# GpSimd runs the S5 parameter chain, with reordered loads, products and sums, in a hybrid decoder layer

## The chip, the cores and the metric

The kernel runs on one core of one Trainium2 chip. The metric is the device time of one execution in microseconds (us). Engines: PE is TensorE (matmul), DVE is VectorE, ACT is ScalarE, POOL is GpSimd, and SP is SyncE, which only issues transfers.

## The reference

One layer of a hybrid decoder with D = 1024 channels and T = 1024 tokens, batch 1, all in float32. x is normalised, projected by one matrix of 4352 columns, and split into an RWKV-7 branch (512 wide, 8 heads of 64), an S5 branch (512 wide, 32 groups of 16 channels, 64 complex states each) and two gates. The branches are merged, projected and added to x; a gated MLP with a causal convolution of width 3 (22 tiles of 128 hidden channels a half) follows.

```python
h = rms_norm(x, norm_mix_pre);  proj = h @ w_in
p_rwkv, u_s5, gates = split(proj);  gates = sigmoid(gates + b_gate)
o_rwkv = rwkv7_branch(p_rwkv, ...) @ w_branch_rwkv     # token shift, decay, delta rule scan, norm, gate
o_s5 = s5_branch(u_s5, ...) @ w_branch_s5
x = x + rms_norm((g_rwkv * o_rwkv + g_s5 * o_s5) @ w_out, norm_mix_post)
h = rms_norm(x, norm_ffn_pre)
f = conv_ffn(h, w_up, conv_w, conv_b, w_down)          # gelu(gate) * val after the convolution
x = x + rms_norm(f, norm_ffn_post)

# s5_branch
lam = a_re + 1j * a_im;  dt = exp(log_step)[:, None]
a_bar = exp(lam * dt)
b_bar = ((a_bar - 1) / lam)[..., None] * (b_re + 1j * b_im)
# states = scan of  s_t = a_bar * s_(t-1) + b_bar u_t ;  y = Re(c . states) + d * u ; gelu ; glu
```

What the change calls the S5 parameter chain is `a_bar`, `(a_bar - 1) / lam` and powers of `a_bar`, per group and state: arrays of 128 partitions by 32.

## The kernel before

**Products.** Float32 is kept by splitting each operand into a rounded high part and a low part, and by three matmuls for each product: high times high, high times low, low times high. Tiles are 128x128 (weights) by 128x512 (half of the tokens). The token halves are th = 0 and 1. The program needs 9040 matmuls. `split` makes the two parts with a cast on ACT (L164, L234) and a subtraction on DVE (L165, L235).

**Order.** PE's order is the order of the program text (`manual_schedule` for PE). In the mixing stage a small planner writes it: *lanes* are generators that yield a cost and a latency, `drive` runs the lane step whose latency is over, and fills the time between with projection products (*background* or *fill*), by the numbers `T_...`, `PACE` and `CREDIT` at the end of the file. The order on DVE, ACT, POOL and SP is a scheduler's, which follows priorities (`high_priority(HP)`, `HP2`, `HPW`, `HPN`: larger goes first). Each engine then runs its own queue strictly in order; a transfer is issued by the engine that is named in the code, and stands in that engine's queue.

**The start.** `start` loads x (8 tiles of 256 KB per half) and four tiles of w_in, twice. For each of 8 blocks k it makes `hh` (ACT, L1015) and `hl` (DVE, L1016), then 4 x 3 products go into the four banks gm (L1083 to L1085). In parallel the squares `sq` of x are summed (ACT L1021, DVE L1023, L1025), PE adds them over partitions (L253), DVE takes a root (`rsy`, L147), PE spreads it (L280) and ACT copies it to `rbc` (L1037). Only with rbc are the four banks of a half evicted (DVE L1047, ACT L1048), and x scaled (L1042). The products of th = 1 reuse the banks. `s5_setup` (`sm` tiles, 128x32; helpers at L332, L334, L339, L344) stands in DVE's queue between these steps; its sine and absolute-value steps run on ACT (L399 to L406), its powers of two are built with an integer conversion (L365). `s5_tables` (L508 on) uses what the chain ends with.

**Later stages.** Input projections go to `shifted` and are stored in DRAM as RKV; `rwkv_front` loads them (L660, tiles ld); `rwkv_level` and others work on 64 small blocks of the delta rule (products into cz and rp banks, copies by ACT L848, L858). `merge`, `outproj` and `mid_norms` end the mixing stage. `fast_up` is the up projection in 22 pairs n; each is built from seven products, of which the last parts are `sixth`, `rest` and `finish`: products 5 and 7 in `rest`, 4 and 3 in `finish`, and a bank `b` that is copied out (`keep`, L1510) after 6, 7 and 4 and then added to further. `down` is the down projection as seven products (`p1` to `p7`), whose operands are sums of cached tiles (S, T, A, B: L1627 adds, L1630 subtracts), with banks b and x evicted between them (`keep1`, `c11`, `keep2`, `c22`, `c21`).

**Banks.** Accumulators are banks of 128x512. `gmp` takes them from the pool of the phase (tag gm, `ngm` of 4 or 2); `chp` from the pool of the phase too.

## Time and profile before

| | |
|---|---|
| median of 3 runs | 1420.2 us (1417.61 to 1421.41) |
| the profiled execution | 1419.13 us, its span 1417.3 us |
| PE busy | 1382.5 us (98%) |
| DVE busy | 1096.4 us (77%) |
| ACT busy | 779.4 us (55%) |
| POOL busy | 79.3 us (6%) |
| mean granted clock of PE | 0.992 |

The span runs from the first to the last instruction of the profiled execution; its time is 1.8 us more. A row of a timeline has the start, the duration (of a run of equal instructions together, with x and their number), the engine, the line of the kernel, the operation, output and inputs, and in brackets how long the engine stood idle before it and what ended that. Matmul rows show the length of the pipeline; how far two starts are apart is the time that one takes. L numbers are lines of the kernel before.

### The profile page before, as it was taken

The numbers are of one execution on the slowest core, as the hardware profiler recorded it, in microseconds if no ns is written. First come the engines' busy times: TensorE is split into PE (matmuls) and PEld (weight loads), VectorE is DVE, ScalarE is ACT, GpSimd is POOL, SyncE is SP. The second block draws the span as 40 slices with busy tenths as digits, with TensorE's granted clock in tenths as the row PEclk, the third lists the DMA queues.
The fourth block names the chain that finished last, engine by engine and source line by source line (L and its number), as shares of the span: only waits on it lengthen the run. The fifth ranks groups of instructions, "written<-read, shape, count | busy, mean of one in ns | idle before, by whom it ended". The sixth has DMA issues, their size and how long they took to land.

```text
span 1417.3 us, 24036 instructions
## 1 busy us (share of the span) xinstructions
PE 1382.5 (98%) x9040; PEld 1123.0 (79%) x9040; DVE 1096.4 (77%) x1847; ACT 779.4 (55%) x1279; POOL 79.3 (6%) x159
## 2 busy tenths in 40 slices
PE   7999999999999999999999999999999999999997
PEld 5767888878877877877787888888888887878885
DVE  7996885376722989667797898988898887598777
ACT  7678878364433555444555565555555554444452
POOL 0000010121000010000000121000000000000000
PEclk9999999999999999999999999999999999999999
DMA  7364444463321474633565866444444437944713
GB/s 243 93 197 134 157 135 134 149 201 127 109 95 62 156 247 134 201 107 106 174 212 172 289 201 193 163 142 164 148 164 156 141 104 261 336 167 154 253 54 120
DMA packets 122501, 232.21 MB, mean 164 GB/s; under 512 B 22144, under 2 KB 28416, under 8 KB 122384
## 3 DMA queue, kind: packets, MB, share of 16 engines
q1 hardware_dynamic: 109456, 190.56, 41.6%
q0 software_dynamic: 11200, 37.82, 7.3%
q10 hardware_dynamic: 1728, 2.29, 0.4%
q8 instruction: 71, 1.16, 0.3%
q14 instruction: 46, 0.38, 0.1%
HBM read 165.60 MB, written 62.91 MB: 161 GB/s over the span
## 4 chain that ended last, share of the span: by engine, by line
PE 49%; issue 21%; DVE 4%; DMA 3%; ACT 2%; POOL 1%; SPq 0%; POOLq 0%; ACTq 0%; DVEq 0%
PE gm L180 7%; PE gm L181 6%; PE gm L182 6%; PE mm L1677 2%; PE mm L1679 2%; PE mm L1678 2%; PE ch L1498 1%; PE ch L1496 1%; PE ch L1497 1%; PE mm L1496 1%; PE mm L1498 1%; PE mm L1497 1%; PE cz L723 1%; DMA st<-in_w_down_dram 1%; PE ch L1678 1%
## 5 line engine op out<-in xcount | busy, mean ns | idle before, releaser
L180 PE MATMUL gm<-hh,wh 128*128 128x512 f32 x672 | 276.3, 411 | 2.5 <-ACT ev L1221 1.5
L181 PE MATMUL gm<-hl,wh 128*128 128x512 f32 x672 | 264.7, 394 | 0.2
L182 PE MATMUL gm<-hh,wl 128*128 128x512 f32 x672 | 264.3, 393 | 0.0
L164 ACT CAST wh<-wf 128x512 fp32r<-128x512 f32 x165 | 101.5, 619 | 132.5 <-PE gm L181 62.3
L165 DVE TENSOR_TENSOR wl<-wf,wh 128x512 fp32r<-128x512 f32 x165 | 112.8, 686 | 75.4 <-ACT wh L164 74.5
L180 PEld LDWEIGHTS gm<-hh,wh 128*128 128x128 f32 x672 | 127.4, 190 | 36.7 <-issue 4.0
L182 PEld LDWEIGHTS gm<-hh,wl 128*128 128x128 f32 x672 | 127.3, 189 | 27.6
L181 PEld LDWEIGHTS gm<-hl,wh 128*128 128x128 f32 x672 | 127.4, 190 | 25.4 <-issue 1.0
L1496 PE MATMUL rp<-t,h 128*128 128x512 f32 x264 | 102.8, 389 | 1.6 <-ACT p L1510 1.6
L1498 PE MATMUL rp<-t,l 128*128 128x512 f32 x264 | 102.7, 389 | 0.0
L1497 PE MATMUL rp<-t,h 128*128 128x512 f32 x264 | 102.7, 389 | 0.0
L1517 DVE SCALAR_TENSOR_TENSOR y<-zv,vecs,y 128x1023 f32<-128x1023 f32 (+1 forms) x44 | 56.4, 1281 | 15.1 <-ACT y L1515 15.0
L1677 PE MATMUL mm<-xh,wh 128*128 128x512 f32 x154 | 60.0, 390 | 0.0
L1679 PE MATMUL mm<-xh,wl 128*128 128x512 f32 x154 | 59.9, 389 | 0.0
L1678 PE MATMUL mm<-xl,wh 128*128 128x512 f32 x154 | 59.9, 389 | 0.0
L1496 PEld LDWEIGHTS rp<-t,h 128*128 128x128 f32 x264 | 49.6, 188 | 12.3 <-ACT p L1510 2.1
L1498 PEld LDWEIGHTS rp<-t,l 128*128 128x128 f32 x264 | 49.5, 188 | 10.5 <-DVE l L235 0.2
L1497 PEld LDWEIGHTS rp<-t,h 128*128 128x128 f32 x264 | 49.5, 188 | 10.2
L235 DVE TENSOR_TENSOR l<-r,h 128x1024 fp32r<-128x1024 f32 x22 | 26.9, 1224 | 21.2 <-ACT h L234 21.2
L234 ACT CAST h<-r 128x1024 fp32r<-128x1024 f32 x22 | 23.2, 1054 | 34.3 <-PE rp L1497 34.3
L234 ACT CAST wh<-S 128x1024 fp32r<-128x1024 f32 (+1 forms) x18 | 17.6, 980 | 40.8 <-PE mm L1678 29.4
L1221 ACT ACTIVATE ev<-gm,hb_b_gate 128x512 f32<-128x512 f32 x32 | 21.9, 686 | 30.7 <-PE gm L182 21.6
(513 smaller groups left out, 3380.3 us busy)
## 6 DMA issues: line engine op xcount, KB each, us to landing
r<-in_w_up_dram SPq DMA_DIRECT2D x44, 512.0 KB, 3.9
wf<-in_w_in_dram SPq DMA_DIRECT2D x62, 256.0 KB, 3.0
st<-in_w_down_dram SPq DMA_DIRECT2D x55, 256.0 KB, 4.5
wf<-in_w_up_dram SPq DMA_DIRECT2D x44, 256.0 KB, 3.2
ACT<-y POOLq DMA_DIRECT2D x22, 512.0 KB, 2.9
st<-ACT SPq DMA_DIRECT2D x40, 256.0 KB, 5.3
GT<-ev SPq DMA_DIRECT2D x32, 256.0 KB, 2.3
wf<-in_w_out_dram SPq DMA_DIRECT2D x32, 256.0 KB, 2.7
```

The source lines that it names most:

```text
L164: nc.scalar.copy(h[:, :n], f[:, :n])
L165: nc.vector.tensor_tensor(l[:, :n], f[:, :n], h[:, :n].bitcast(F32), ALU.subtract)
L180: mm(ps, a, xh[k], start=k == 0, stop=False)
L181: mm(ps, a, xl[k], start=False, stop=False)
L182: mm(ps, b, xh[k], start=False, stop=k == n - 1)
L1496: mm(ps, wh[:, c], xh, start=first and k == 0, stop=False, skip_group_check=True)
L1497: mm(ps, wh[:, c], xl, start=False, stop=False, skip_group_check=True)
L1498: mm(ps, wl[:, c], xh, start=False, stop=k == len(xs) - 1, skip_group_check=True)
L1517: V.scalar_tensor_tensor(y[:, lag:], z[:, 0:1024 - lag], self.vec(nme, i), y[:, lag:], ALU.mult, ALU.add)
L1677: mm(ps, wh[:, c], xh[:, x], start=start, stop=False, skip_group_check=True)
L1678: mm(ps, wh[:, c], xl[:, x], start=False, stop=False, skip_group_check=True)
L1679: mm(ps, wl[:, c], xh[:, x], start=False, stop=stop, skip_group_check=True)
```

## The change

1. `s5_setup` runs on POOL (`nc.gpsimd`) instead of DVE; its fused steps (`scalar_tensor_tensor`) become two. The reciprocal and the integer conversions stay on DVE, with priority HPN. ACT's sine and absolute-value steps are unchanged.
2. HPN goes from 500000 to 900000, so the loads of `start` are issued ahead of the first weight tiles (L163). `ones1` and a zero tile are set first, ACT is given one small activation at once, and 11 products of the zero tile stand in front of the first real one.
3. The gm banks come from two pools, one of which spans all phases; `chp` uses the same ones; the order of the two kinds in the tail is swapped.
4. In `rwkv_level` products and copies of each of the two sets d are written together, with a shorter yield after each; nine of the planner's numbers differ, PACE and CREDIT among them.
5. RKV and YU stores are issued by POOL instead of SP; the loads of `rwkv_front` of th = 0 by SP instead of POOL.
6. `s5_unit` takes its last four tiles in plain order.
7. In the last pair of `fast_up`, product 7 and its copy stand before product 5, and the copy (`keep`) has priority HP2. The first operands of `down` are issued after that copy.
8. In `down`, the evictions and their sums have priority HP2.

```diff
     def gmp(self):
         if self.tail:
             self.flip = not self.flip
-            return self.mmp() if self.flip else self.chp()
-        return self.ps.tile([128, 512], F32, tag="gm", name=self.nm("gm"), bufs=self.ngm)
+            return self.chp() if self.flip else self.mmp()
+        self.flip = self.ngm > 2 and not self.flip
+        return (self.ps if self.flip else self.psg).tile([128, 512], F32, tag="gm", name=self.nm("gm"), bufs=2)
-    def chp(self, par=None):
-        tag = "ch" if par is None else f"ch{par}"
-        return self.ps.tile([128, 512], F32, tag=tag, name=self.nm("ch"), bufs=2)
+    def chp(self):
+        return self.psg.tile([128, 512], F32, tag="gm", name=self.nm("ch"), bufs=2)
...
+        nc.scalar.activation(xp.tile([128, 1], F32, name="table"), self.ones1, AF.Identity, scale=self.ones1)
...
     def s5_setup(self):
-        nc, V = self.nc, self.nc.vector
+        nc, V = self.nc, self.nc.gpsimd
...
             def stt(x, sc, y, o0, o1):
-                z = sm()
-                V.scalar_tensor_tensor(z, x, sc, y, o0, o1)
+                z = ts(x, sc, None, o0)
+                V.tensor_tensor(z, z, y, o1)
                 return z
...
-                    V.tensor_scalar(i, kk, 127.0, 2.0 ** 23, ALU.add, ALU.mult)
+                    with self.tc.high_priority(HPN):
+                        nc.vector.tensor_scalar(i, kk, 127.0, 2.0 ** 23, ALU.add, ALU.mult)
...
-            V.reciprocal(rd, d1)
+            with self.tc.high_priority(HPN):
+                nc.vector.reciprocal(rd, d1)
...
-        nc.sync.dma_start(ys.rearrange("j c g n -> (j c) g n"), y8)
+        nc.gpsimd.dma_start(ys.rearrange("j c g n -> (j c) g n"), y8)
...
-            (nc.sync if th else nc.gpsimd).dma_start(t, src[:, o])
+            nc.sync.dma_start(t, src[:, o])
...
@@ rwkv_level, both halves
-        for p, xz in zip(P, Z):
-            for u in range(2):
                 for h in range(2):
                     A.copy(xz[hi[h], u], p[u][hi[h], 0])
-        yield 1.6, T_LV
+            yield 0.8, T_LV if d is ds[1] else 0
...
@@ start
+        for _ in range(NWARM):
+            nc.tensor.matmul(sums[1][:, 0:128], self.zero, self.zero, start=True, stop=True)
...
-                self.nc.sync.dma_start(self.RKV[mt][:, th * 512:th * 512 + 512], y)
+                self.nc.gpsimd.dma_start(self.RKV[mt][:, th * 512:th * 512 + 512], y)
...
@@ s5_unit
-        for m, th in [(m, th) for m in range(6) for th in range(2)] + [(6, 1), (7, 1), (6, 0), (7, 0)]:
+        for m, th in [(m, th) for m in range(NK) for th in range(2)]:
...
@@ fast_up, keep
-            A.copy(t, ps)
+            with self.tc.high_priority(HP2):
+                self.kept = A.copy(t, ps)
...
@@ fast_up, rest
-            self.product(d["c"], d["w"][5], xs[5], True)
+            if n < FT - 1:
+                self.product(d["c"], d["w"][5], xs[5], True)
             self.product(d["b"], d["w"][7], xs[7], False)
             u3 = keep(n, 2, d["b"])
+            if n == FT - 1:
+                self.product(d["c"], d["w"][5], xs[5], True)
...
@@ down, p1
-                o = operands(g, cA[g], b)
+                if g:
+                    o = operands(g, cA[g], b)
+                else:
+                    with self.tc.issue_after(self.kept.ins):
+                        o = operands(g, cA[g], b)
...
@@ down, c11 (keep1, keep2, c22 and c21 likewise)
-            add(f[0][m], f[0][m], x[m])
+            with self.tc.high_priority(HP2):
+                add(f[0][m], f[0][m], x[m])
...
-T_US, T_TAB0, T_TAB, T_TRIG, T_SCAN = 4.12, 35.94, 16.96, 16.21, 24.93
+T_US, T_TAB0, T_TAB, T_TRIG, T_SCAN = 2.49, 35.94, 16.96, 16.21, 24.93
...
-PACE, CREDIT = 0.89, 2.0
+PACE, CREDIT = 1.01, 3.02
+NWARM = 11
...
-HPW, HPN = 400000, 500000
+HPW, HPN = 400000, 900000
```

**How it moves instructions.** ACT's queue in the start, from the last squares of th = 1 to the eviction of the first banks (`sm` is the chain, `rbc` the scale of th = 0). Before:

```order
L1021 ACTIVATE sq_583<-x_262 128x512
L1021 ACTIVATE sq_589<-x_263 128x512
L1037 COPY rbc_531<-chk_307 128x512
L1048 COPY ev_551<-ev_550 128x512
L1048 COPY ev_559<-ev_558 128x512
L1048 COPY ev_567<-ev_566 128x512
L234 CAST hh_610<-x_248 128x512
```

Now:

```order
L1022 ACTIVATE sq_601<-x_269 128x512
L403 ACT_TABLE_LOAD
L403 ACTIVATE sm_979<-sm_977 128x32
L404 ACTIVATE sm_981<-sm_977 128x32
L410 ACTIVATE sm_985<-sm_986 128x32
L405 ACTIVATE sm_980<-sm_981,hpi 128x32
L403 ACTIVATE sm_1051<-sm_1049 128x32
L404 ACTIVATE sm_1053<-sm_1049 128x32
L1022 ACTIVATE sq_607<-x_270 128x512
L405 ACTIVATE sm_1052<-sm_1053,hpi 128x32
L1038 COPY rbc_549<-chk_314 128x512
L1049 COPY ev_569<-ev_568 128x512
```

The table load and the seven steps of the chain, which came 15 rows behind rbc, now come ahead of it.

PE's queue in the last pair of `fast_up` (n = 21): rp is bank `b`, filled by product 7, copied by `keep` and then added to by product 4; mm is the bank of product 5. Where product 7 ends, before:

```order
L1496 MATMUL rp_12326<-t_9798,h_2256_12231 128x512
L1497 MATMUL rp_12326<-t_9799,h_2256_12231 128x512
L1498 MATMUL rp_12326<-t_9798,l_2257_12232 128x512
L1496 MATMUL rp_12326<-t_9376,h_2256_12231 128x512
L1497 MATMUL rp_12326<-t_9377,h_2256_12231 128x512
L1498 MATMUL rp_12326<-t_9376,l_2257_12232 128x512
```

Now:

```order
L1499 MATMUL rp_12366<-t_9838,h_2256_12271 128x512
L1500 MATMUL rp_12366<-t_9839,h_2256_12271 128x512
L1501 MATMUL rp_12366<-t_9838,l_2257_12272 128x512
L1499 MATMUL mm_12425<-t_9398,h_2254_12266 128x512
L1500 MATMUL mm_12425<-t_9399,h_2254_12266 128x512
L1501 MATMUL mm_12425<-t_9398,l_2255_12267 128x512
```

Before, product 4 follows product 7 in the same bank at once; now the twelve matmuls of product 5 lie between.

DVE's queue in `down`, from the operands of the third product to the first of the four sums `p` that free the banks x (S, T, A, B are cached operands, st loaded ones, wl and xl low parts). Before:

```order
L1627 TENSOR_TENSOR S_12759<-S_12759,st_12991 128x1024
L1627 TENSOR_TENSOR S_12800<-S_12800,st_13031 128x1024
L235 TENSOR_TENSOR wl_2382_12996<-S_12759,wh_2381_12995 128x1024
L235 TENSOR_TENSOR xl_2384_12998<-T_12506,xh_2383_12997 128x1024
L1627 TENSOR_TENSOR S_12839<-S_12839,st_13071 128x512
L1630 TENSOR_TENSOR T_12506<-B_13003,T_12506 128x1024
L1627 TENSOR_TENSOR S_12867<-S_12867,st_13097 128x1024
L1630 TENSOR_TENSOR S_12759<-S_12759,A_12501 128x1024
L1627 TENSOR_TENSOR p_2330_12719<-p_2330_12719,rp_12496 128x512
L235 TENSOR_TENSOR wl_2388_13036<-S_12800,wh_2387_13035 128x1024
L1627 TENSOR_TENSOR p_2331_12727<-p_2331_12727,rp_12497 128x512
```

Now:

```order
L1634 TENSOR_TENSOR S_12799<-S_12799,st_13031 128x1024
L235 TENSOR_TENSOR wl_2382_13036<-S_12799,wh_2381_13035 128x1024
L235 TENSOR_TENSOR xl_2384_13038<-T_12546,xh_2383_13037 128x1024
L1634 TENSOR_TENSOR S_12840<-S_12840,st_13071 128x1024
L1637 TENSOR_TENSOR T_12546<-B_13043,T_12546 128x1024
L1634 TENSOR_TENSOR S_12879<-S_12879,st_13111 128x512
L1637 TENSOR_TENSOR S_12799<-S_12799,A_12541 128x1024
L1634 TENSOR_TENSOR p_2330_12759<-p_2330_12759,rp_12536 128x512
L235 TENSOR_TENSOR wl_2388_13076<-S_12840,wh_2387_13075 128x1024
L1634 TENSOR_TENSOR p_2331_12767<-p_2331_12767,rp_12537 128x512
```

One sum of 128x1024 (S<-S,st) that stood ahead of the first p now stands behind the four.

More of the change, by code (lines that the diff above doesn't have):

```diff
@@ L288, in setup @@
         nc.scalar.dma_start(self.vecs, self.a["vec"])
+        self.ones1 = self.const.tile([128, 1], F32, name="ones1")
+        nc.gpsimd.memset(self.ones1, 1.0)
+        self.zero = xp.tile([128, 128], F32, name="zero")
+        nc.gpsimd.memset(self.zero, 0.0)
         raw = xp.tile([128, 4, 32], F32, name="s5raw")
@@ L1386, in mid_norms @@
         nc = self.nc
-        yield 0, T_N0
+        yield 0, T_N6 if th else T_N0
         ss = self.rp()
@@ L1745, in keep2 @@
             f[1][m] = ft(f"q{m}")
-            A.copy(f[1][m], b[m])
+            with self.tc.high_priority(HP2):
+                A.copy(f[1][m], b[m])
         def c22(m):
             y = f[1][4 + m] = ft(f"r{m}")
-            A.copy(y, b[m])
-            add(y, y, x[m])
-            add(x[m], x[m], f[1][m])
+            with self.tc.high_priority(HP2):
+                A.copy(y, b[m])
+                add(y, y, x[m])
+                add(x[m], x[m], f[1][m])
         def c21(m):
             y = f[0][4 + m] = ft(f"s{m}")
-            A.copy(y, b[m])
+            with self.tc.high_priority(HP2):
+                A.copy(y, b[m])
             squares(0, y)
```

22 lines of the change are left out of this document (11 added, 11 removed).

## The prediction

> **What bounds the kernel now.** I read the page first (its part 1), then the list of waits of the matrix engine (PE), then windows and the timeline at the places that the list names.
>
> ```profile
> PE 1382.5 (98%) x9040; PEld 1123.0 (79%) x9040; DVE 1096.4 (77%) x1847; ACT 779.4 (55%) x1279; POOL 79.3 (6%) x159
> ```
>
> PE is busy for 98% of a span of 1417.3 us, so PE's own work is the bound, and a change that leaves its products alone can win only what PE waits, or what its clock loses after a wait. The list of waits (us in total, times, longest) says how much that is and where:
>
> ```profile
> PE gm L1083 <- ACT wh L234: 9.0, 1, 9.0
> PE gm L1160 <- ACT ev L1166: 2.7, 3, 1.3
> PE cz L854 <- issue: 2.1, 1, 2.1
> PE rp L1496 <- ACT p L1510: 1.6, 1, 1.6
> PE rp L764 <- DVE sv L693: 1.5, 1, 1.5
> PE rp L1677 <- DVE p L1627: 1.4, 1, 1.4
> PE mm L180 <- ACT mx L1373: 1.0, 1, 1.0
> ```
>
> One wait of 9.0 us stands before the first product, and the other six rows add up to 10.3 us. The windows (length, then PE, PEld, DVE, ACT and POOL busy with counts, PE's granted clock, the share of the DMA engines, GB/s) add two things: vector engine (DVE) time is scarce near the start, and behind two of the waits the clock is down.
>
> ```profile
> 0.00:20.00 20.00, 9.93 (x28) 7.36 (x29) 14.31 (x56) 12.49 (x22) 1.19 (x10) 1.00 0.82 265
> 80.00:100.00 20.00, 17.34 (x71) 12.10 (x69) 19.59 (x39) 14.79 (x27) 0.82 (x2) 1.00 0.53 174
> 380.00:430.00 50.00, 47.94 (x910) 37.48 (x909) 13.96 (x23) 19.91 (x47) 0.00 (x0) 0.93 0.31 102
> 480.00:530.00 50.00, 48.23 (x440) 38.56 (x439) 43.89 (x88) 28.09 (x57) 6.48 (x12) 0.93 0.76 249
> 7.70:34.80 27.10, 24.45 (x97) 19.26 (x98) 25.12 (x67) 23.29 (x41) 0.00 (x0) 1.00 0.76 248
> ```
>
> DVE is busy 19.59 of 20 us in 80 to 100 and 25.12 of 27.10 in 7.7 to 34.8. A clock of 0.93 over 50 us is some 3.5 us lost beside the wait itself, in each of the two windows.
>
> **The start.** Timelines of PE, of the SP queue, of ACT and of DVE (start, duration, instruction), and among them the page's row on the transfers of w_in (KB, us from issue to landing):
>
> ```profile
> 8.98 0.79 PE L1083 MATMUL gm<-hh,wh 128*128 128x512 f32 x1 [8.98 <-ACT wh L234]
> ...
> 14.61 0.63 PE L1083 MATMUL gm<-hh,wh 128*128 128x512 f32 x1
> 15.04 0.63 PE L1084 MATMUL gm<-hl,wh 128*128 128x512 f32 x1
> ...
> 17.73 0.39 PE L1083 MATMUL gm<-hh,wh 128*128 128x512 f32 x1
> 17.95 0.39 PE L1084 MATMUL gm<-hl,wh 128*128 128x512 f32 x1
> ```
> ```profile
> 0.74 0.86 SPq L163 DMA_DIRECT2D wf<-in_w_in_dram  x2
> 1.64 0.43 SPq L994 DMA_DIRECT2D x<-in_x_dram  x1
> ```
> ```profile
> wf<-in_w_in_dram SPq DMA_DIRECT2D x62, 256.0 KB, 3.0
> ```
> ```profile
> 6.40 1.28 ACT L1015 ACT_TABLE_LOAD   x1 [6.40 <-DMA x<-in_x_dram]
> ...
> 34.80 0.59 ACT L1037 COPY rbc<-chk 128x512 f32<-128x512 f32 x1 [0.15 <-PE chk L280]
> ...
> 55.36 0.23 ACT L399 ACTIVATE sm<-sm 128x32 f32<-128x32 f32 x1 [3.52 <-DVE sm L334]
> ```
> ```profile
> 6.56 0.19 DVE L339 TENSOR_TENSOR sm<-s5raw 128x32 f32<-128x32 f32 x1 [0.93 <-DMA s5raw<-in_s_a_dram]
> ...
> 7.37 0.19 DVE L339 TENSOR_TENSOR sm<-s5raw 128x32 f32<-128x32 f32 x1
> ```
>
> The first x goes out behind two weight tiles (0.74, 1.64), ACT loads its table only when x is there (6.40, 1.28 us), the first product starts at 8.98, and the second block of twelve (k=1) at 14.61. Up to there products are 0.43 apart, later 0.22 to 0.23.
>
> In the new order x is the first transfer. It has the size of a w_in tile, 256 KB, which takes 3.0 us to land, so it is there at 0.74 + 3.0 = 3.7 and not at 6.40: 2.7 earlier. The table is in by then (1.28), so the first product comes at about 8.98 - 2.7 - 1.3 = 5.0. Four weight tiles follow; at the 265 GB/s of the first window one takes 1.0, the fourth is there at 7.7, its cast and split take 0.6 and 0.7, and k=1 comes at about 9 instead of 14.61. Eleven zero products ahead of it keep PE warm, so that the 0.43 becomes 0.23. That is 5.6 us at k=1.
>
> It is not 5.6 us later on. The copy rbc (34.80), behind which the banks of the first half are evicted, is in ACT's queue behind 23.29 us of work in the window 7.70 to 34.80. It could now begin near 4.0 instead of 7.7. But the order puts a table load (1.28) and seven small sine and absolute-value steps in front of rbc; they stood behind it (55.36). I price them at 1.28 + 7 x 0.2 = 2.7 (0.23 is one of them by the row at 55.36). ACT's idle time in that window, 27.10 - 23.29 = 3.8, shrinks too, by half I assume. So rbc comes at 34.8 - 3.7 - 1.9 + 2.7 = 31.9, and PE, ready sooner, waits for it at the first bank. **Term 1: -3** (bounds -5.6, if that queue cost nothing, and +5, below).
>
> **The chain on GpSimd (POOL).** What it cost and what it will cost, by groups of DVE in the first 110 us, a window of DVE that holds little else (busy us, count), and groups of POOL over the run:
>
> ```profile
> L339 DVE TENSOR_TENSOR sm<-sm,sm 128x32 f32<-128x32 f32 x25 | 4.0, 183 | 0.1
> L235 DVE TENSOR_TENSOR hl<-x,hh 128x512 fp32r<-128x512 f32 x16 | 10.4, 684 | 0.8 <-ACT hh L234 0.8
> ```
> ```profile
> 53.00:57.90 4.90, 4.90 (x52) 1.00 0.14 48
> ```
> ```profile
> L635 POOL TENSOR_TENSOR rkb<-csts,vecs 128x128 f32<-128x128 f32 x4 | 1.5, 408 | 0.0
> L461 POOL MEMSET s5ar<- 128x32 f32 x1 | 0.1, 143 | 0.0
> ```
>
> On DVE a 128x32 step is 183 ns long but overlaps the next, 52 of them in 4.9 us, so some 145 steps were about 14 us. On POOL no 128x32 product is in the trace: 408 ns for 128x128 is an upper bound, 143 ns for a memset of 128x32 a lower one; I take 0.25 a step, near the lower end since the width is the memset's, with 0.05 for the wait of each on its predecessor. 144 steps from 7.3 (the second raw tile is used on DVE at 7.37) are then 36 us, done by 43, well ahead of the tables made from them near 87. On the way, DVE's exponent steps (L369) need the chain's 45th and 48th steps, at 7.3 + 48 x 0.25 = 19.3, and stand in DVE's queue ahead of the operands of k=4, due at 9 + 3 x 2.7 = 17.1 (twelve products of 0.225 a block). ACT's sines need the 75th, at 26, and ACT is there at about 28. The first is 2.2 us late, which rbc hides; the second is 2 us early.
>
> Contention decides how sure that is. Tile q at the very end, where both engines add two SBUF tiles (least, median and longest ns of one), and the two timelines:
>
> ```profile
> L1730 DVE TENSOR_TENSOR q<-q,A x3: 679/693/1289, 1409.9 to 1412.5; 128x512 f32<-128x512 f32 x3
> ```
> ```profile
> 1409.40 1.25 POOL L1730 TENSOR_TENSOR q<-q,A 128x512 f32<-128x512 f32 x1
> ```
> ```profile
> 1409.91 1.89 DVE L1730 TENSOR_TENSOR q<-q,A 128x512 f32<-128x512 f32 x2
> ```
>
> One of three equal DVE adds took 1289 instead of 693 ns. It began at 1409.91, POOL's add ended at 1410.65, and 1289 is 0.74 of waiting and 0.55 of work: here DVE waited until POOL was done. The Trainium skill, "SBUF — State Buffer", section "SBUF: two separate sides", says that the port pair the two share is an exclusive lock, taken by whichever starts first for its whole instruction, and that a DVE operation with two SBUF inputs is blocked by a GpSimd one that reads SBUF; by that rule nearly each of these 144 steps would meet a DVE split or sum at the start, and Term 1 would be the +5 of the slower rival instead of -3, and the sum -0.7 with all else equal. The trace agrees in this one instance.
>
> My reason for not taking that as the likeliest is that the steps are short: 0.2 us each, 144 x 0.2 = 29 us spread over a period in which DVE gets 14 us back, so the balance over the start is -14 to +15, and its middle is nothing on DVE. What I count in Term 1 is the earlier data, not DVE time.
>
> **The waits after the start.** The three of L1160 are for banks whose eviction on ACT and DVE is late; one of them:
>
> ```profile
> 91.30 0.50 PE L1160 MATMUL gm<-lx,lw 128*128 128x512 f32 x1 [1.19 <-ACT ev L1166]
> ```
>
> With DVE freed of the steps that it had at 53 and with banks shared over both pools, I take 2.0 of the 2.7 of L1160. **Term 2: -2** (0 to -2.7).
>
> **Stores and loads.** The rkv and yu stores go to POOL's queue, the rwkv loads of the first half to SP's. POOL's queue is in order: the first store stands behind the whole chain and a memset of kpad. The first was due here on SP:
>
> ```profile
> 84.04 0.33 SPq L1190 DMA_DIRECT2D RKV<-ev  x1
> ```
>
> The chain is done at 43 (estimate), 41 us ahead, so I cost this at nothing; a chain of twice that length would just hold it.
>
> **The RWKV stage.** At L854 PE stood 2.06 us with nothing to wait for in the trace:
>
> ```profile
> 398.12 0.91 PE L854 MATMUL cz<-gr,ld 32*32 32x32 f32 x46 [2.06 <-issue]
> ```
>
> The products of a level are now issued for one of the two sets in hand and copied, then for the other, so copies lie beside products. But "issue" is no copy, so I take 1 of 2.1 (0 to -5.6, with the clock). At L764 (1.5, -5 with the clock) the order around the sums changes, and I take 1. **Terms 3 and 4: -1 and -1.** The bank pool removes the wait at L180 for mx, which was for a bank of a phase that ended. **Term 5: -1.0** (0 to -1).
>
> **The last pair and the sums.**
>
> ```profile
> 1181.84 0.50 PE L1496 MATMUL rp<-t,h 128*128 128x512 f32 x1 [1.63 <-ACT p L1510]
> ```
> ```profile
> 1248.88 0.47 PE L1677 MATMUL rp<-xh,wh 128*128 128x512 f32 x1 [1.43 <-DVE p L1627]
> ```
> ```profile
> 1246.92 1.22 DVE L1630 TENSOR_TENSOR S<-S,A 128x1024 f32<-128x1024 f32 x1
> ```
>
> At 1181.84 PE waits for a copy of the bank that its last product filled. Twelve matmuls of product 5 come in between in the new order, 12 x 0.225 = 2.7 us, and the wait was 1.63. **Term 6: -1.6** (0 if the copy is held behind ACT's cast, which its priority excludes). At 1248.88 PE waits for the first sum, behind DVE's queue of wide operands. In the new order one wide sum (1.22, by the row at 1246.92, about 1.1 apart) less stands ahead of it. **Term 7: -1.1** (0 to -1.4). The split that stood behind that sum (wl<-S) still stands right behind it, so it comes no later than before.
>
> **New waits.** Nine planner values change, and products shift by tens of places in the mixing phase. Every such move can open a wait like those in the list, whose smaller ones are 1.0 to 1.6: I take two small ones, less cover. **Term 8: +2** (0 to +6).
>
> **Sum.** -3 - 2 - 1 - 1 - 1 - 1.6 - 1.1 + 2 = -8.7, from the profiled run's 1419.1 (span 1417.3, 1.8 around it) to 1410.4. The median of the three runs is 1.1 higher, so the forecast against it is 1420.2 - 8.7 = 1411.5, and I say 1411.
>
> **Rivals.** *More than the waits.* The clock losses at 400 and 500 go with their waits (3.5 each, by the 0.93), and another 2 with a small wait: 1411 - 8 = 1402 or so. For it speaks that both follow a wait of 1.5 us or more at once; against it, that L854 was waiting for nothing shown.
>
> *The start gives nothing.* POOL's steps cost as much DVE time as they free and delay the sines by 5 us or so: Term 1 becomes +2, Term 2 nothing. -1.7 in all, 1418.5, no change.
>
> *Slower.* Each POOL step meets a DVE split and waits for it (0.6 apart, 684 ns long), then holds DVE for 0.2: 0.8 a step. DVE then reaches its exponent steps at 16 when POOL has done about 13 of 48, idles until 16 + 35 x 0.25 = 24.7, and its operands for k=4 come 8 us late. POOL does the next 27 steps partly against DVE, and ACT holds rbc for the sines until about 39.5 instead of 34.8: +5. What remains of the chain, 70 steps x 0.2, takes 14 us of DVE where it is full, of which I put 4 on PE. 5 + 4 - 5.7 (Terms 3 to 7) + 2 = +5.3: 1425.5. The point from which rbc is held is 0.28 us a step, (28.4 - 7.3) / 75; slower than before by the whole, from about 0.4. For it speaks the 1289 row; against it, that one instance is between 1.25 us instructions.
>
> **Chances.** Forecast 0.47; more 0.13; the start gives nothing 0.24; slower 0.16. Faster or slower by 0.3% is 4.3 us, which is about what a measurement can tell. Of the forecast's own range, 1405 to 1416, nearly all is faster (0.45), of the start that gives nothing a quarter (0.06), with more 0.13: faster 0.64. Slower 0.15 and the rest 0.21. The range takes in half of the first rival and reaches to the edge of the slower one, 1401 to 1424.
>
> **What would show it.** First product below 6.5 us and k=1 below 10; the chain on POOL at 0.25 a step and over before 50; DVE splits at 684 ns as before; rbc at 31 to 33, sines ending before it; no PE row of 1 us at L1160; no waits at the last pair and at the first sum; PE idle of less than 15 us in all. It would be wrong if POOL steps are 0.4 or more apart, if DVE's two-input rows have means above 800 ns, if rbc is after 35, or if a new wait of 2 us or more stands in the mixing phase.

## The result: slower by 0.7%, and the profile after

The changed kernel takes 1428.9 us (median of 6 runs, 1426.7 to 1431.5) against 1418.2 (6 runs, 1417.4 to 1421.4): ratio 1.0069, 95% interval 1.0054 to 1.0083. The profiled execution is the shortest of the six: 1426.7, span 1424.9, mean clock 0.990.

Part 1 of the page and the list of PE's waits, as shown of before:

```profile
PE 1386.6 (97%) x9062; PEld 1125.9 (79%) x9062; DVE 1086.0 (76%) x1727; ACT 782.7 (55%) x1282; POOL 144.8 (10%) x310
```
```profile
PE gm L1087 <- DVE hl L1017: 7.8, 2, 7.5
PE gm L180 <- DVE ev L1048: 4.7, 1, 4.7
PE gm L1163 <- DVE last L1112: 3.0, 1, 3.0
PE chk L253 <- DVE sq L1026: 1.9, 1, 1.9
PE rp L769 <- DVE ld L743: 1.7, 1, 1.7
PE ch L1688 <- ACT xh L234: 1.3, 1, 1.3
...
PE ch L1689 <- DVE xl L235: 0.8, 1, 0.8
```

The 9.0 in front of the first product is gone, and so are the rows of L1496, L1677 and mx. The product of L854 is L857 now and waits 0.4; that of L764 is L769 now and still waits, 1.7 for another tile. Four others stand at the top, all in the first 110 us, and each is a wait for DVE. The windows (same columns as before) say the same:

```profile
0.00:20.00 20.00, 17.68 (x71) 13.72 (x71) 8.69 (x21) 13.78 (x23) 13.24 (x44) 1.00 0.92 322
20.00:40.00 20.00, 11.43 (x38) 9.06 (x39) 15.06 (x32) 11.04 (x19) 18.10 (x43) 0.74 0.34 109
...
380.00:430.00 50.00, 49.62 (x844) 39.45 (x843) 22.65 (x49) 20.40 (x47) 0.00 (x0) 1.00 0.38 123
480.00:530.00 50.00, 47.70 (x447) 38.10 (x446) 45.14 (x87) 27.73 (x56) 5.39 (x10) 1.00 0.68 231
```

From 20 to 40 us PE is busy 11.43 of 20 at a clock of 0.74, while DVE, the scarce engine, is busy for only 15.06, and POOL for 18.10. Later, the two windows that had 0.93 have 1.00.

To place the loss, I give every matmul its length at full clock (0.227 us for 128x512), add these up in PE's order without the zero products, and compare the times at which two kernels reach the same sum. In us behind the profiled run of before (minus: ahead), at so many us of work done:

| kernel | 5 | 15 | 30 | 50 | 65 | 80 | 140 | 300 | 460 | 740 | 1120 | 1300 |
|---|---|---|---|---|---|---|---|---|---|---|---|---|
| changed kernel | -6.3 | 6.8 | 7.4 | 14.2 | 13.8 | 16.2 | 17.4 | 13.8 | 6.6 | 8.8 | 9.5 | 7.2 |
| chain_on_pool_only | -2.9 | 13.8 | 15.0 | 15.0 | 15.6 | 15.8 | 15.6 | 15.5 | 13.2 | 15.3 | 15.1 | 15.0 |
| conversions_low | -6.0 | -3.8 | 7.3 | 21.1 | 20.8 | 22.0 | 23.2 | 19.6 | 13.6 | 18.4 | 20.9 | 18.6 |
| chain_on_dve | -2.7 | -2.6 | -2.5 | -2.2 | -2.6 | 2.0 | 3.1 | -0.5 | -7.9 | -7.1 | -6.9 | -9.2 |
| chain_awaited_by_none | -5.9 | -4.8 | -4.3 | -3.8 | -4.2 | 7.8 | 9.5 | 5.9 | 0.0 | 3.1 | 3.7 | 2.0 |
| chain_free_of_queues | -4.4 | -3.1 | -2.8 | -2.3 | -2.7 | 3.1 | 4.6 | 1.0 | -3.8 | -0.7 | -0.5 | -2.8 |
| early_loads_only | -1.4 | -1.3 | -1.2 | -1.0 | -1.4 | 1.9 | 2.2 | 2.6 | 2.8 | 2.1 | 2.1 | 1.1 |
| late_parts_only | -0.5 | -0.5 | -0.5 | -0.5 | -0.7 | 1.7 | 2.6 | -0.3 | -5.3 | -1.9 | -0.9 | -2.3 |
| first_block_loads_early | -2.9 | -2.5 | -2.4 | -2.1 | -2.5 | -2.1 | 0.3 | -3.3 | -7.8 | -4.0 | -3.5 | -5.7 |

The first row has the whole result: 6.3 ahead after the first products, 17.4 behind at 140 us of work, and then 10.2 won back. The start loses in steps, at about 10, 50 and 80 us of work. The timelines show the first two (start, duration, instruction, in brackets the idle time ahead of it and what ended that): PE, DVE, POOL and ACT.

```profile
18.75 0.39 PE L1086 MATMUL gm<-hh,wh 128*128 128x512 f32 x1
26.64 0.79 PE L1087 MATMUL gm<-hl,wh 128*128 128x512 f32 x1 [7.50 <-DVE hl L1017]
...
28.09 0.63 PE L1087 MATMUL gm<-hl,wh 128*128 128x512 f32 x1
28.52 0.63 PE L1088 MATMUL gm<-hh,wl 128*128 128x512 f32 x1
```
```profile
14.48 0.74 DVE L235 TENSOR_TENSOR wl<-u,wh 128x512 fp32r<-128x512 f32 x1
23.88 0.21 DVE L369 TENSOR_SCALAR sm<-sm 128x32 int32<-128x32 f32 x1 [8.65 <-POOL sm L335]
...
25.85 0.74 DVE L1017 SCALAR_TENSOR_TENSOR hl<-x,vecs,hh 128x512 fp32r<-128x512 f32 x1
```
```profile
20.51 2.37 POOL L335 TENSOR_SCALAR sm<-sm 128x32 f32<-128x32 f32 x7
...
25.47 1.27 POOL L335 TENSOR_SCALAR sm<-sm 128x32 f32<-128x32 f32 x2
```
```profile
42.38 0.30 ACT L405 ACTIVATE sm<-sm,hpi 128x32 f32<-128x32 f32 x1
42.59 0.56 ACT L1038 COPY rbc<-chk 128x512 f32<-128x512 f32 x1
...
68.80 1.26 ACT L1148 CAST lw<-wf 64x512 fp32r<-64x512 f32 x2 [10.82 <-POOL s5ai L483]
70.08 0.58 ACT L1038 COPY rbc<-chk 128x512 f32<-128x512 f32 x1
```

DVE comes to the integer conversion (L369) at 15.2 and stands 8.65 us for the chain on POOL, with the low parts hl of the next block queued behind; PE starts its last product at 18.75. After that wait its products are 0.43 apart, not 0.23, until 30. The squares behind the conversion are late too: ACT stands for them, and PE 1.9 at L253. The first rbc comes at 42.59 (34.80 before). ACT does not wait for the chain's sines ahead of it, only for the squares:

```profile
ACT sq L1022 <- DVE sq L1026: 8.5, 2, 8.2
```

At 58 ACT comes to lw, the cast of the low-rank weights: the tile lies in the memory of the chain's temporaries, and waits 10.82 for the chain's last use of them. The second rbc stands behind, 70.08, PE waits 4.72 for a bank, again followed by products 0.43 apart. The third step is the 3.0 at L1163.

POOL's steps are about 0.36 apart at 20.51 (seven in 2.37) while DVE stands, and nearly twice that at 25.47 (the third starts at 26.82), as DVE works again. DVE's own splits are hardly longer than before, where they had a mean of 684 ns:

```profile
L235 DVE TENSOR_TENSOR hl<-x,hh 128x512 fp32r<-128x512 f32 x16 | 10.7, 696 | 0.8 <-ACT hh L234 0.8
```

### The profile page after: what moved, and what is told of

Its sections match the earlier page's. It is cut to its first block, busy times and chain, and to the rows that moved or that the text cites. A ratio compares the mean times of both kernels' runs of the same rounds, so it can differ in the third digit from the quotient of the medians.

```text
span 1424.9 us, 24092 instructions
## 1 busy us (share of the span) xinstructions
PE 1386.6 (97%) x9062; PEld 1125.9 (79%) x9062; DVE 1086.0 (76%) x1727; ACT 782.7 (55%) x1282; POOL 144.8 (10%) x310
## 4 chain that ended last, share of the span: by engine, by line
PE 80%; issue 6%; POOL 4%; DVE 3%; ACT 3%; DMA 2%; SPq 0%; ACTq 0%; POOLq 0%; DVEq 0%
PE gm L180 9%; PE gm L181 8%; PE gm L182 8%; PE rp L1501 4%; PE rp L1500 4%; PE rp L1499 4%; PE mm L1499 4%; PE mm L1500 4%; PE mm L1501 4%; PE mm L1688 2%; PE mm L1689 2%; PE mm L1690 2%; PE ch L1499 1%; PE ch L1501 1%; PE ch L1500 1%
## 5 line engine op out<-in xcount | busy, mean ns | idle before, releaser
L182 PE MATMUL gm<-hh,wl 128*128 128x512 f32 x672 | 263.7, 392 | 0.0
L182 PEld LDWEIGHTS gm<-hh,wl 128*128 128x128 f32 x672 | 127.0, 189 | 27.6
L1521 DVE SCALAR_TENSOR_TENSOR y<-zv,vecs,y 128x1023 f32<-128x1023 f32 (+1 forms) x44 | 56.4, 1281 | 15.1 <-ACT y L1519 15.1
L1499 PEld LDWEIGHTS rp<-t,h 128*128 128x128 f32 x264 | 49.5, 188 | 10.5 <-ACT rp L1536 0.2
L1501 PEld LDWEIGHTS rp<-t,l 128*128 128x128 f32 x264 | 49.6, 188 | 10.2
L1565 POOL DMA_DIRECT2D ACT<-y x22 | 11.7, 533 | 313.6 <-DVE y L1564 290.9
L235 DVE TENSOR_TENSOR l<-r,h 128x1024 fp32r<-128x1024 f32 x22 | 26.9, 1223 | 20.9 <-ACT h L234 20.9
```

The source lines that it names most:

```text
L182: mm(ps, b, xh[k], start=False, stop=k == n - 1)
L1499: mm(ps, wh[:, c], xh, start=first and k == 0, stop=False, skip_group_check=True)
L1501: mm(ps, wl[:, c], xh, start=False, stop=k == len(xs) - 1, skip_group_check=True)
L1521: V.scalar_tensor_tensor(y[:, lag:], z[:, 0:1024 - lag], self.vec(nme, i), y[:, lag:], ALU.mult, ALU.add)
```

## Experiments

Theory A: a dependent step on POOL costs 0.36 us alone and waits for DVE's two-input adds, one add a step; DVE itself is hardly slowed; and PE loses only where DVE or ACT wait in order for the chain. Theory E (a part of the slower rival of the prediction): each step of POOL also holds DVE.

| kernel | median us (range, runs) | ratio to before, 95% |
|---|---|---|
| chain_on_dve | 1416.2 (1410.3 to 1422.1, 10) | 0.9983, 0.9964 to 1.0003 |
| chain_on_pool_only | 1432.9 (1431.9 to 1434.5, 4) | 1.0105, 1.0090 to 1.0120 |
| conversions_low | 1433.4 (1430.5 to 1438.2, 4) | 1.0111, 1.0086 to 1.0135 |
| lowrank_after_scale | 1430.2 (1425.6 to 1430.8, 4) | 1.0086, 1.0070 to 1.0103 |
| chain_behind_start | 1422.5 (1418.1 to 1428.5, 10) | 1.0027, 1.0011 to 1.0043 |
| late_parts_only | 1417.0 (1409.4 to 1420.6, 10) | 0.9978, 0.9961 to 0.9996 |
| early_loads_only | 1420.3 (1417.5 to 1425.2, 10) | 1.0012, 0.9998 to 1.0026 |
| chain_awaited_by_none | 1421.4 (1416.2 to 1427.3, 12) | 1.0029, 1.0013 to 1.0046 |
| chain_free_of_queues | 1419.1 (1416.6 to 1423.7, 11) | 1.0012, 1.0001 to 1.0023 |
| first_block_loads_early | 1413.9 (1408.4 to 1417.9, 12) | 0.9962, 0.9947 to 0.9977 |
| no_zero_products | 1418.2 (1416.4 to 1422.9, 10) | 1.0006, 0.9993 to 1.0019 |

The runs of a kernel with parts 3 to 8 spread over 5 to 12 us. A single profile can therefore stand some us off its median; the profiled run of chain_on_dve is its shortest (1410.3).

**Which part does it.** Three runs: the changed kernel with the chain back on DVE, the kernel before with the chain alone moved, and the kernel before with parts 3 to 8 alone.

```diff
 chain_on_dve (against the changed kernel; fused steps and plain conversions again)
-        nc, V = self.nc, self.nc.gpsimd
+        nc, V = self.nc, self.nc.vector
 chain_on_pool_only (against before; steps split, conversions on DVE with HPN)
-        nc, V = self.nc, self.nc.vector
+        nc, V = self.nc, self.nc.gpsimd
 late_parts_only (against the changed kernel; the chain as in chain_on_dve, no zero tile, no early table load)
-NWARM = 11
+NWARM = 0
-HPW, HPN = 400000, 900000
+HPW, HPN = 400000, 500000
```

> The changed kernel with the S5 chain back on DVE (fused steps, conversions and reciprocal at the chain's own priority); all other parts of the change stay. Theory A (in-order queues of DVE and ACT stall on the slow POOL chain in the first 110 us): the 17.4 us by which PE lies behind at 140 us vanish, plus about 1.5 for the earlier data: about 1410, PE idle of 7.5 us before the k=4 operands and 4.7 us before the first product after the start gone. Theory B (the new load order, the warm products or the new planner numbers are what costs): stays at 1424 or more.

> The kernel before with only the S5 chain moved to POOL (split steps, conversions and reciprocal on DVE at the top priority). Theory A: the same stalls without the other parts, PE 15 to 20 us behind at 140 us, about 1433 to 1440. Theory B: within 3 us of 1418.

> The kernel before with the parts 3 to 8 of the change (banks, level products, planner numbers, stores and loads, last pair, sums) and without the parts 1 and 2 (chain on DVE, old load order, no early table load, no zero products). Theory A: PE level with before at 140 us, 10 us ahead at the end of the profiled run: 1408 to 1413. Theory G (what the later parts win in one trace they lose to the clock in the next run): 1414 to 1419.

The chain alone on POOL costs 1.05%, more than the whole change, and in the changed kernel taking it back wins 1.0069 / 0.9983 = 0.9% or 12 us. Its 1416.2 is 6 above the 1410 expected, which the profiled run alone reaches, and far below theory B's 1424. Parts 3 to 8 alone win 0.22% (0.04 to 0.39); their 1417.0 lies in the range of theory G, not in theory A's 1408 to 1413. Waits of PE, DVE and ACT in chain_on_pool_only:

```profile
PE gm L1086 <- DVE hl L1018: 6.1, 1, 6.1
...
DVE sm L366 <- POOL sm L332: 9.4, 2, 9.0
...
ACT sm L400 <- POOL sm L334: 13.9, 1, 13.9
```

PE's lag goes from -2.9 to 15.0 between 5 and 30 us of work, and rises by less than 1 after that: the same conversion, and the sines on ACT, 13.9, with the next hh behind them.

**Moving the first wait.** The conversions get the chain's own, lower priority.

```diff
-                    with self.tc.high_priority(HPN):
-                        nc.vector.tensor_scalar(i, kk, 127.0, 2.0 ** 23, ALU.add, ALU.mult)
+                    nc.vector.tensor_scalar(i, kk, 127.0, 2.0 ** 23, ALU.add, ALU.mult)
```

> The changed kernel with the four conversions and the reciprocal of the chain at the chain's own priority instead of the top one, so that in DVE's queue the second pair no longer stands ahead of the operands of k=4. Theory A1 (the chain is slowed most while DVE is busy, and only moves while DVE waits): the 8.65 us wait of DVE goes, but the chain then runs at 0.6 to 0.7 a step, ACT's sines hold rbc to 42 or later as before, total within 4 us of 1429. Theory A2 (the DVE wait itself is the cost, 7.5 us and the half clock behind it): 1416 to 1419.

```profile
PE gm L180 <- DVE ev L1046: 10.5, 1, 10.5
PE gm L1084 <- DVE ev L1046: 8.7, 2, 8.5
...
ACT sm L402 <- POOL sm L337: 9.7, 2, 8.2
```

The first stall is gone (3.8 ahead at 15 us of work instead of 6.8 behind), and the wait comes back larger at rbc: ACT stands 8.2 for the sines, then 16.6 for lw, and PE waits 8.5 and 10.5 for banks. The chain itself ends at 77.9 instead of 72.2, since its conversions come later. Removing one queue's wait moved it to the next. Theory A2 is refuted; the time is 4.5 above the changed kernel's, a little outside A1's 4.

**Moving the second wait.** lw behind the second rbc.

```diff
-                nc.scalar.copy(w[a][sl], f[sl])
+                with self.tc.issue_after(self.spread_done.ins):
+                    nc.scalar.copy(w[a][sl], f[sl])
```

> The changed kernel with the casts of the low-rank weights (lw), which wait for memory that the chain's last steps hold, placed behind the copy of the second scale (rbc, th=1) in ACT's queue. Theory A: the 10.8 us wait of ACT before lw no longer holds rbc, the 4.7 us wait of PE after the start and its half clock go: about 1422. Theory C (the second scale is late by itself, since the products before it are late): 1428 to 1429.

The second rbc comes at 64.6 instead of 70.1, but lw still stands ahead of hh on ACT (4.5 for POOL there), and PE's wait at that bank is 3.8 instead of 4.7. The 1422 of theory A did not come. The profiled run, the shortest of four, is 1.1 below that of the changed kernel; the other three took 1430.2 to 1430.8. Nothing is won that the times could show.

**The price of a step by itself.** A kernel that computes only chains of alternating multiply and add steps of 128x32 on POOL, alone and beside DVE adds, in place of the layer.

```python
G.tensor_scalar(y, last, 0.5, None, ALU.mult)      # POOL, 128x32, then
G.tensor_tensor(w, y, z[:, 0:32], ALU.add)         # the next needs it
V.tensor_tensor(o, src[:, 0:512], g[:, 512:1024], ALU.add)   # DVE beside it: src is SBUF (both) or PSUM (psum)
```

> Leaves the layer out. In turn: 24 dependent POOL steps of 128x32 alone (multiply by a number, then add two tiles), 24 DVE adds of 128x512 with two SBUF inputs alone, both side by side, the DVE adds with one input from PSUM alone and beside POOL steps, and DVE adds of 128x64 alone and beside POOL steps. Theory A (POOL waits for the DVE instruction that runs): 0.33 to 0.36 us a POOL step alone, 0.6 to 0.75 beside the wide two-SBUF adds, with DVE lengthened by under 0.1 an add; beside the PSUM adds as alone. Theory D (POOL's steps are slow by themselves, and the lengthening in the layer is something else): 0.33 to 0.36 in every stretch. Theory E (as predicted: DVE is what waits): DVE adds lengthened by 0.2 or more for each step.

Its groups by shape (busy us, mean ns): POOL beside DVE adds of two SBUF tiles (both) and beside adds with a PSUM input (psum), and DVE's adds in the two stretches.

```profile
L1848 DVE TENSOR_TENSOR vboth<-z,gate 128x512 f32<-128x512 f32 x40 | 25.0, 699 | 0.0
L1848 DVE TENSOR_TENSOR vwps<-ps,gate 128x512 f32<-128x512 f32 x40 | 24.0, 675 | 0.0
...
L1838 POOL TENSOR_SCALAR both<-both 128x32 f32<-128x32 f32 x11 | 6.7, 608 | 1.0
...
L1841 POOL TENSOR_TENSOR both<-both,z 128x32 f32<-128x32 f32 x12 | 5.9, 492 | 1.0
...
L1838 POOL TENSOR_SCALAR psum<-psum 128x32 f32<-128x32 f32 x11 | 3.2, 289 | 1.0
...
L1841 POOL TENSOR_TENSOR psum<-psum,z 128x32 f32<-128x32 f32 x12 | 3.0, 252 | 1.0
```

The stretch meant for POOL alone was not alone: DVE's adds began at 7.48, after its first three steps, which were 0.34 to 0.37 apart. With 0.08 to 0.09 between two steps (1.0 in 11 or 12), a step is 0.36 beside PSUM adds, the same as those three, and 0.64 beside SBUF adds, which is one DVE add. DVE's adds there start 0.635 apart, and 0.602 once POOL is done. So the step waits for the add, and the add loses 0.03: theory A. The Trainium skill, "SBUF — State Buffer", section "SBUF: two separate sides", has an exclusive lock on the shared ports that the first to start holds for its whole instruction; the runs agree that the two exclude each other only where DVE has two SBUF inputs. In the cases here each side's loss goes with the length of the other's instructions: 0.3 us steps against 0.6 us adds cost POOL 0.28 a step and DVE 0.03 an add; against adds of 128x64, 0.135 apart alone, they cost POOL 0.02 (0.38 apart) and DVE 0.015 (0.151 apart); and the 1.25 us add at the very end cost DVE 0.6.

**A POOL chain that nobody awaits.** The conversions go to POOL too, the sines behind the second rbc, lw behind the start's last hh.

```diff
-                    with self.tc.high_priority(HPN):
-                        nc.vector.tensor_scalar(i, kk, 127.0, 2.0 ** 23, ALU.add, ALU.mult)
+                    V.tensor_scalar(i, kk, 127.0, 2.0 ** 23, ALU.add, ALU.mult)
...
-                nc.scalar.activation(si, x, AF.Sin)
+                with self.tc.issue_after(self.rbc_done.ins):
+                    nc.scalar.activation(si, x, AF.Sin)
...
-                nc.scalar.copy(w[a][sl], f[sl])
+                with self.tc.issue_after(self.ev_done.ins):
+                    nc.scalar.copy(w[a][sl], f[sl])
```

> The changed kernel with the chain wholly on POOL (the integer conversions too), and with nothing that ACT or DVE needs soon queued behind it: ACT's sine and absolute-value steps are issued behind the second rbc (th = 1), and the casts lw, whose memory the chain's tiles hold, behind the start's last hh. Theory A (POOL's steps take 0.36 us alone and 0.64 beside DVE's adds, DVE is hardly slowed, and the loss comes only from queues that wait in order for the chain): DVE has no idle of 8 us before 25, first rbc at 31 to 34 instead of 42.6, no PE stall at 18.8 and at 69.8; PE is 3 to 6 us ahead of the kernel before up to 50 us of work; the chain ends between 78 and 92, and since the tables on DVE need it near 87, a wait of up to 5 us may stand there. Time 1412 to 1420. Theory E (each POOL step takes DVE time): DVE's splits come 0.1 to 0.2 later each, PE is 5 or more behind by 50 us of work although nobody waits for the chain, and the time stays at 1423 or more.

Up to 65 us of work the forecast of theory A holds: the first rbc is at 30.4, and PE is 4 to 6 us ahead with the chain running on POOL all the time. That refutes theory E for this stretch. The time missed by 1.4 us: lw still came before the chain's end at 81.

```profile
PE gm L180 <- ACT wh L164: 6.0, 1, 6.0
```
```profile
ACT lw L1153 <- POOL s5ai L484: 11.1, 1, 11.1
```

ACT's 11.1 hold the casts of the next weights, PE's 6.0 wait for these, and the lag goes from -4.2 to 7.8 by 80 us of work. The last run gave lw memory of its own, and took the load order of first_block_loads_early (below) as well.

```diff
-        w = [self.lrp.tile([128, 512], F32R, name=self.nm("lw"), tag=f"lw{a}") for a in range(2)]
+        w = [self.lwp.tile([128, 512], F32R, name=self.nm("lw"), tag=f"lw{a}") for a in range(2)]
```

> The chain wholly on POOL as in the run in which nobody awaited it, and two things more: the low-rank weights lw get memory of their own, so that ACT's casts of them no longer wait for the chain's tiles (11.1 us there), and only the first x tile and four w_in tiles go ahead of the weight tiles. Some of the chain's tiles share memory, so that all fits. Theory A (only in-order waits cost): no wait of ACT for POOL of over 2 us in the first 110 us, PE's wait at 80 to 87 for the weights (6.0) is below 1, PE is 3 to 6 us ahead of the kernel before up to 65 us of work and still 1 us or more ahead at 100, and the time is 1410 to 1416, as good as with the chain on DVE or a little better. Rival (work on POOL at this time costs PE 5 us or more by a way not seen in the waits): PE is behind at 100 us of work without such a wait, and the time is 1418 to 1423.

The wait for the weights is gone, and at 65 us of work PE was still 2.7 ahead. Then DVE, in its timeline, stands for the tables that the chain ends with, the copies of the low-rank banks wait behind, and PE after them:

```profile
78.61 0.29 DVE L526 TENSOR_TENSOR sml<-s_b,s5q 128x128 f32<-128x128 f32 x1 [4.01 <-POOL s5ai L485]
...
85.41 0.15 DVE L1119 COPY last<-gm 128x1 f32<-128x1 f32 x1
```
```profile
85.70 0.47 PE L1171 MATMUL gm<-lx,lw 128*128 128x512 f32 x1 [1.45 <-DVE last L1119]
```

5.8 are lost between 65 and 80 us of work, and 1419.1 is within the rival's 1418 to 1423, though not by its way: the lag comes behind this wait, which my expectation had not named. The chain on POOL ends at 83, and there the real users stand. It is 0.5% behind the same loads with the chain on DVE. That other orders of the tables would win it back was not tried.

**The loads, and a later chain on DVE.**

```diff
 early_loads_only (before with part 2 alone: also the table load, the zero tile and its 11 products)
-HPW, HPN = 400000, 500000
+HPW, HPN = 400000, 900000
```

> The kernel before with part 2 of the change only (data loads first, early table load, 11 zero products). Theory A: 2 to 3 us ahead from 20 us on, 1415 to 1417. Theory B: slower than before.

> The changed kernel with the chain on DVE, its first exponential held until the low part of x block 3 is issued, so that the start's operands come first. Theory A: the first product at 5.5 and the second without a wait for hl, PE 5 to 6 us ahead at 30 us and still 3 to 5 ahead at 60; 1408 to 1412 by the median, against chain_on_dve. Theory F (the second half of the start is held by rbc and by DVE whatever comes first): at most 3 us ahead at 60, 1414 to 1418.

```diff
 chain_behind_start (against chain_on_dve; held: lo of block 3)
-            s1, s2, q = exp_parts(ls)
+            with self.tc.issue_after(self.held.ins):
+                s1, s2, q = exp_parts(ls)
```

early_loads_only has its first product 3.5 earlier, keeps 1 to 1.4 of it up to 65 us of work, and loses 3.3 there; the 1415 to 1417 expected did not come (1420.3). The same wait of PE stands in chain_on_dve, whose rows of PE and of the SP queue are:

```profile
PE gm L182 <- DVE wl L165: 3.8, 1, 3.8
```
```profile
24.33 2.75 SPq L163 DMA_DIRECT2D wf<-in_w_in_dram  x4
```

The first weight tiles went out at 0.74 before, and go out at 24.33 behind all the loads of the start. They are not late for that: ACT casts the first four from 46.39 to 59.26, as in first_block_loads_early (below). But the queues behind are ordered otherwise. DVE splits the third and fourth at 68.49 (59.38 there), the next two tiles go out at 69.20 (by 61 there), and the wl for which PE waits is made only at 85.53.

chain_behind_start (1422.5) missed both ranges. Its chain ends late on DVE, and ACT stands for the memory of lw once more, with no POOL in it; the split of the weights comes after that, and PE's wait at L182 is 10.6:

```profile
ACT lw L1149 <- DVE s5ai L482: 5.3, 1, 5.3
```

> The changed kernel with the chain on DVE, where only the first x tile and the first four w_in tiles go ahead of the weight tiles (L163), not all of the start's loads; table load, zero products and parts 3 to 8 as changed. Theory L (what the early loads win at the first block, 3.5 us, is lost at 65 to 70 us of work because the first weight tiles then stand behind 4 MB of x and w_in): the wait of L182 for wl (3.8 in two earlier runs) is below 1, PE stays 2 to 4 us ahead of the kernel before from the first block to 100 us of work, and the time is 1411 to 1416. Rival (the 3.5 us are lost at the first bank eviction, since rbc does not come earlier): lag returns to 0 by 50 us of work, and the time is 1416 to 1419, as with all loads early.

```diff
-        load_x(0, 0)
+        with self.tc.high_priority(400000):
+            load_x(0, 0)
...
-                load_w(b, i)
+                with self.tc.high_priority(0 if i else 400000):
+                    load_w(b, i)
...
-HPW, HPN = 400000, 900000
+HPW, HPN = 400000, 500000
```

```profile
4.48 0.91 SPq L163 DMA_DIRECT2D wf<-in_w_in_dram  x2
```
```profile
PE gm L1163 <- ACT ev L1169: 3.5, 2, 1.9
```

The weights go out at 4.48, the wait for wl is gone, and PE keeps its 2 to 2.5 us up to 80 us of work; then the old wait of the low-rank banks (3.5) takes them. 1413.9 is the best of all kernels, 0.38% below before. Its interval overlaps that of all loads early (0.9983), so the gain over these rests on the lag, not on the times. The two differ in priorities alone. HPN at 900000 raises all of `start`, its steps on ACT and DVE as well as its loads; this run raises only the loads of the first block. So the wait for wl goes with the order that HPN makes; that the loads alone make it is not shown.

```diff
 no_zero_products (against chain_on_dve)
-NWARM = 11
+NWARM = 0
```

> The changed kernel with the chain on DVE and without the 11 products of the zero tile in front. Theory (they only bring PE to full clock before the first real product): products stand about 0.43 apart for the first 3 to 4 us instead of 0.22, the second block is up to 2 us later, and since rbc at 34 is what the first banks wait for, the time is unchanged within 2 us (1415 to 1419). Rival (the slow start is carried on): 2 to 4 us more, 1419 to 1421.

Without the eleven zero products PE is 1.5 ahead at 50 us of work instead of 2.2, a difference of 0.7. It is small since with them, too, products stood 0.43 apart, from 10.12 to 13.10, behind a wait of 2.55 for hl. Later the wait for wl is 6.8 in this trace and 3.8 in chain_on_dve. The times do not resolve any of it: 1418.2 is 2.0 above chain_on_dve, with overlapping intervals.

## Why the prediction was wrong

The forecast was -8.7 and the traces show +7.2 at equal work. By its terms:

- **The chain's price, the step that failed.** 0.25 a step was taken near the memset's end of its bounds. It was 0.36 alone, inside the bounds of 0.143 to 0.408, and 0.64 beside DVE, outside them. The first step began at 5.2, so at 0.36 the 45th alone ends at 5.2 + 45 x 0.36 = 21.4, 6 us after DVE asks for it (the conversion began at 23.88). The prediction had that condition right (rbc held from 0.28 a step, slower from 0.4) and put the price on the wrong side of it. It also weighed the contention as DVE time (-14 to +15), while DVE's splits went only from 684 to 696 ns: the chain paid. Of its own signs of being wrong, steps 0.4 or more apart and rbc after 35 came; means above 800 ns on DVE did not.
- **"2.2 us late, which rbc hides."** The wait was 8.65, and PE ran dry behind its product at 18.75, long before rbc matters; and rbc came at 42.59, not 31.9, since the squares stood behind that wait too.
- **Term 1, -3 with Term 2, -2.** Together they were to give -5; PE is 17.4 behind at 140 us of work. The first product came at 5.74 (forecast 5.0) and the first block's gain of 6.3 was real (forecast 5.6 at k=1): what was said of loads, table and warm PE held. 13.1 were lost at the conversion, 6.8 at lw, 3.2 at L1163 and around. No term named lw: the text spoke of DMA queues behind the chain, not of memory that the chain's tiles hold. Term 2's wait stayed, 3.2 at L1163 against 2.7.
- **The slower rival** had the places (DVE idle 16 to 24.7, measured 15.2 to 23.9; rbc 39.5, measured 42.6) and the step's wait for DVE (0.6, measured 0.64). But it let each step hold DVE for 0.2 more, measured 0.03, and had rbc wait for the sines, where the squares were what came late. Hence it saw 4 us on DVE later that did not come, missed the second stall, and stopped at 1425.5.
- **Stores and loads at nothing: held.** No engine waits for a store of RKV in the first 110 us. The chain was over at 72, not 43, before the 84 at which the first store had been due.
- **Terms 3 and 4, -2.** From 300 to 460 us of work the lag goes from 13.8 to 6.6: -7.2, in late_parts_only -5.0. The clock of both windows is 1.00, but the waits themselves are mostly still there. L854's 2.1 is 0.4 in this trace, yet the same product waits 0.9 to 1.8 in late_parts_only, chain_on_dve and first_block_loads_early, which have part 4 too; L764's 1.5 is 1.7 (0.9 to 2.2 in the others). So by these traces most of the size is the lost clock, which the text had only in its bounds and in the rival "more than the waits".
- **Term 5, -1.** The wait for mx, 1.0 at 694 us, is gone, but one of 1.1 (et at L253) stands in its place at 703, and from 460 to 740 us of work the lag rises by 2.2. Not won. What the text had not seen is a gain earlier, from 140 to 300 us of work: -3.6, in late_parts_only -2.9. The idle time of the window that holds it is gone:

```profile
250.00:330.00 80.00, 80.00 (x504) 66.79 (x503) 47.42 (x72) 44.50 (x67) 11.85 (x26) 1.00 0.50 171
```

  Before, it had 78.52 of 80 at a clock of 0.98: 1.5 of waits for evictions, which the text had not listed, and the clock again. Whether the bank pool did it is not shown.
- **Term 6, -1.6.** The wait for the copy is gone, but 1.3 (xh) and 0.8 (xl) stand a little later at the head of `down`, whose operands are now issued behind that copy. PE's lag between 740 and 1120 us of work rises by 0.7. Moved, not won.
- **Term 7, -1.1.** From 1120 to 1180 the lag falls by 2.2. But it falls as much in early_loads_only, which has not this part, so the part is not shown to be its cause.
- **Term 8, +2.** The new waits after the start are 1.3, 0.8, 0.6 (L694) and the 1.1 at L253; a second 1.1 there stood before as well. Terms 3 to 8 were to give -3.7 and gave -10.2 in this trace, -4.9 in late_parts_only, whose times say -0.22% (about 3 us) with all its start.

The sum of the misses: +22.4 at the start (17.4 for -5), -6.5 later (-10.2 for -3.7), together the +15.9 between -8.7 and +7.2. By the times the parts add only roughly: +1.05%, +0.12% and -0.22% give +0.95% for the measured +0.69% (0.54 to 0.83).

What stays open: how much of the start's loss beyond the waits is clock rather than late data, since the stretches at half rate differ between runs; whether the planner's numbers or the banks brought most of the later gain; and how much of that gain is this trace's luck, since the profiled run is the shortest of its six.

## What to carry to other kernels

Work moved to an idle engine is free only if every queue that takes its results can come late: before moving it, list each consumer's place in its in-order queue and the due time there, and each tile that will reuse the memory, and price the step with the dependent latency of the new engine beside the busy neighbour. If the first wait is only moved back, it reappears at the next consumer. A priority that puts loads first can reorder other queues as well; bring forward just the tiles that the first products need.

## What was not expected of the hardware

A dependent 128x32 step on POOL is 0.36 us apart, where 52 of the chain's steps on DVE, interleaved, took 4.9 us (0.094 apart). Beside DVE adds of two SBUF tiles it is 0.64, one add each, and the adds lose 5% (0.602 to 0.635); beside adds with a PSUM input neither loses anything. After PE's waits of 7.5 and 4.7 us its products stood 0.43 apart for about 3.5 us (26.64 to 30.22, 74.89 to 78.35), and then 0.23 again. A wait of only 1.9 was followed by such a stretch too (34.77 to 36.90).
